# A pool that stays open into the down projection, two activation tiles loaded as a weight unit, and stores moved later

## The chip, the core and the metric

The kernel runs on one core of one Trainium2 chip. The metric is the time of one execution in device microseconds (us), and the kernel before and the changed kernel are compared by the median of several runs.

## What is computed

One layer of a diffusion backbone over 1024 tokens of width 1024, all in 32-bit floats. Three token mixers run side by side, are merged and projected, and a gated MLP with a depthwise convolution follows. The change concerns the second half only:

```python
x_mix = x + m_lat[:, :, 2] * merge_branches(ya, yb, yc, gates, w_branch[l], w_out[l])
h = rms_norm(x_mix, norm_ffn[l]) * (1.0 + m_lat[:, :, 4]) + m_lat[:, :, 3]
x = x_mix + m_lat[:, :, 5] * conv_ffn(h, w_up[l], w_dw[l], b_dw[l], w_down[l])
# conv_ffn: a, g = split(dwconv(h @ w_up)); return (a * silu(g)) @ w_down
return rms_norm(x, norm_final)
```

The MLP is 2816 wide, that is 22 tiles of 128 channels. Its activation `a * silu(g)` is a 2816 x 1024 array.

## The kernel before

Every large product is made of three products: a 32-bit operand is split into a high part (a cast on ScalarE) and a low part (source minus high part, a subtraction on VectorE), and TensorE multiplies high by high, high by low and low by high. One such matmul has 512 columns.

A weight unit (`w_unit`, L166) is one 512 KB load into a raw tile `wr`, the cast to `wh` and the subtraction to `wl`. Each of the three tags has a ring of three buffers, so a unit waits for the release of the unit three places before it. All loads and stores are issued by one engine, SyncE (SP), in the order of its queue: an issue that waits holds back all issues behind it.

The code is written in program order; a scheduler of the framework puts each engine's instructions into an order at build time. It takes the ready instruction of the smallest number, numbers rise with the program order, and `tc.high_priority(offset=n)` makes an instruction count as n places earlier. An SBUF pool is a stretch of memory, opened on a stack at the left or the right side; a tile of a new pool waits for the tiles that lay on its bytes before (`reuse_waits="tile"`).

The stages that matter here, in order:

- Merge and output projection (`merge_up`, `wo_half`, L656): two halves of 512 tokens. `wo_half` loads the residual tile `xr` (ring of two), adds, stores `xm_d`, and sums squares. `h_tile` makes the normalised input `blk["11"]`, `["21"]`, `["12"]`, `["22"]` on the right side (pool `f2`).
- Up projection (L726 to L844). Tiles f = 0 and 1 are plain, tiles 2 to 21 take seven half-size products (`up_first`, `up_rest`) with sums of the input, `T1`, `T2`, `T3` (pool `tp`, left side, which also holds the convolution's weights `cw`). `act_out` (L686) applies the convolution, SiLU and the gate to one tile: ScalarE L695, VectorE L701, L704, ScalarE L708, VectorE L711. Its operands and results are tiles of tag `c`, a ring of five in the pool `pc`, four for each f. At its end L712 stores the tile to DRAM (`act_d`).
- Down projection (L896 to L957). Pool `p2` is opened where `tp` and `pc` lay, and pool `pa` where the inputs of the up projection lay. `act` (L858) loads one half tile of 512 tokens from `act_d` into `st` (ring of four) and splits it into one of 25 `ac` tiles. The loop runs over two token halves tb, two halves of output channels mh (the last part is done apart, L929 on), 11 weight units f2_ and two tiles in each. A pair f2_ takes 24 matmuls (L871 to L873). The residual `xt` is loaded at the start of each tb.

Of the kernel before, what the change touches and what calls it, by code (L numbers as in the profile page):

```python
# [9 lines left out]
F32 = mybir.dt.float32  # L10
F32R = mybir.dt.float32r
# [7 lines left out]
P = 128  # L19
D = 1024  # L20
KT = D // P
# [9 lines left out]
FT = D_FF // P  # L31
# [6 lines left out]
NC = 5  # L38
# [4 lines left out]
WPRIO = 60  # L43
CTX_POOL = (('v', 1), ('b', 2), ('v', 2), ('b', 3), ('v', 3))
WPRIO_C = 30
WM = 8
WAT = 2
MPRIO = 100
# [43 lines left out]
def build(tc, ins, out, dbg=None):  # L92
    nc = tc.nc
    V, A, G, T, SP = nc.vector, nc.scalar, nc.gpsimd, nc.tensor, nc.sync
    with ExitStack() as top:
# [68 lines left out]
        wprio = [0]  # L164

        def w_unit(src, nk, ncol, lo_eng=None):  # L166

            cnt[0] += 1
            n = nk * ncol
            with tc.high_priority(offset=wprio[0]):  # L170
                raw = wp.tile([P, 1024], F32, tag="wr", name=f"wr{cnt[0]}", bufs=WR)
                SP.dma_start(raw[:, :n], src)
                hi = wp.tile([P, 1024], F32R, tag="wh", name=f"wh{cnt[0]}", bufs=WH)
                lo = wp.tile([P, 1024], F32R, tag="wl", name=f"wl{cnt[0]}", bufs=WL)
                A.copy(hi[:, :n], raw[:, :n])  # L175
                (lo_eng or V).tensor_tensor(out=lo[:, :n], in0=raw[:, :n], in1=hi[:, :n].bitcast(F32),  # L176
                                            op=ALU.subtract)
            return (hi[:, :n].rearrange("p (k n) -> p k n", k=nk),
                    lo[:, :n].rearrange("p (k n) -> p k n", k=nk))
# [440 lines left out]
        with ExitStack() as sm:  # L620
            mp = Aligned(sm.enter_context(tc.tile_pool(name="mp", bufs=2, reuse_waits="tile")))
            merge_up(nc, mp, ins, gate_d, y_d, xm, half, w_unit, gemm_cm, mm2)
        tss = ExitStack()
        tp = Aligned(tss.enter_context(tc.tile_pool(name="tp", bufs=1, reuse_waits="tile")))
        cw = tp.tile([P, 2 * FT, 4], F32, tag="cw", name="cw")
        SP.dma_start(cw, ins["conv"])

        for nm in ("T3", "T1", "T2"):
            blk[nm] = tuple(tp.tile([P, KQ, LH], F32R, tag=f"{nm}{p}", name=f"{nm}{p}") for p in "hl")
        ffs = ExitStack()  # L630
        ff = Aligned(ffs.enter_context(tc.tile_pool(name="ff", bufs=2, reuse_waits="tile")))

# [23 lines left out]
        def wo_half(hf):  # L656

            cols = slice(hf * LH, hf * LH + LH)
            ss = []
            for i in range(KT):  # L660
                w = w_unit(ins["w_out"][i], KT, P)
                z = bank("b", f"wo{hf}{i}", (P, 512))
                for k2 in range(2):
                    gemm_cm(z, [p[:, k2 * KQ:(k2 + 1) * KQ] for p in w], blk["12"[k2] + "12"[hf]], slice(0, LH),
                            first=k2 == 0, last=k2 == 1)
                xr = ff.tile([P, 512], F32, tag="o", name=f"xr{hf}{i}", bufs=2)
                SP.dma_start(xr, ins["xT"][i * P:(i + 1) * P, cols])
                V.scalar_tensor_tensor(out=xm[i][:, cols], in0=z, scalar=mods[:, 0, i:i + 1], in1=xr,
                                       op0=ALU.mult, op1=ALU.add)
                if i > 0:  # L670
                    SP.dma_start(xm_d[hf, i - 1], xm[i - 1][:, cols])
                sumsq(ff, ss, xm[i][:, cols], i, f"m{hf}", 512, 4)
            SP.dma_start(xm_d[hf, KT - 1], xm[KT - 1][:, cols])
            return rms_row(ff, ss, 512, f"m{hf}", "a")
# [3 lines left out]
            h_tile(k, 0, rp)  # L678
        rp = wo_half(1)
        ffs.close()  # L680
        pcs = ExitStack()
        pc = Aligned(pcs.enter_context(tc.tile_pool(name="pc", bufs=1, reuse_waits="tile")))
        P1 = [None]


        def act_out(f, cc_):  # L686

            us = []
            for s in (1, 0):
                c_ = s * FT + f  # L690
                u = pc.tile([P, L], F32, tag="c", name=f"u{f}{s}", bufs=NC)
                o = 0
                for z in cc_[s]:
                    n = z.shape[-1]
                    A.activation(u[:, o:o + n], z, AF.Identity, scale=cw[:, c_, 1:2], bias=cw[:, c_, 3:4])  # L695
                    o += n
                o = 0
                for z in cc_[s]:
                    n = z.shape[-1]
                    e = min(n, L - 1 - o)  # L700
                    V.scalar_tensor_tensor(out=u[:, o + 1:o + 1 + e], in0=z[:, :e], scalar=cw[:, c_, 0:1],  # L701
                                           in1=u[:, o + 1:o + 1 + e], op0=ALU.mult, op1=ALU.add)
                    e = 0 if o else 1
                    V.scalar_tensor_tensor(out=u[:, o + e - 1:o + n - 1], in0=z[:, e:], scalar=cw[:, c_, 2:3],  # L704
                                           in1=u[:, o + e - 1:o + n - 1], op0=ALU.mult, op1=ALU.add)
                    o += n
                if s:
                    A.activation(u, u, AF.Silu)  # L708
                us.append(u)
            g_, a_ = us  # L710
            V.tensor_tensor(out=a_, in0=a_, in1=g_, op=ALU.mult)  # L711
            SP.dma_start(act_d[f], a_)  # L712

        def plain(zs, ws, hf, ks):
# [26 lines left out]
        for k in range(KQ):  # L741
            h1, h2 = xm[k], xm[k + KQ]
            b = {nm: [p[:, k] for p in blk[nm]] for nm in ("T1", "T2", "T3")}
            V.tensor_tensor(out=h1[:, t1], in0=h1[:, t2], in1=h1[:, t1], op=ALU.subtract)
            split(b["T1"], h1[:, t1])
            V.tensor_tensor(out=h1[:, t2], in0=h2[:, t2], in1=h1[:, t2], op=ALU.subtract)
            split(b["T3"], h1[:, t2])
            V.tensor_tensor(out=h2[:, t2], in0=h2[:, t2], in1=h1[:, t1], op=ALU.subtract)
            split(b["T2"], h2[:, t2])
            V.tensor_tensor(out=h2[:, t1], in0=h2[:, t1], in1=h2[:, t2], op=ALU.subtract)  # L750
        act_out(1, za)

        blk["T4"] = blk["12"]
# [54 lines left out]
            return z  # L808

        def up_rest(f, z, w):  # L810
            p1 = P1[0]
            ca, cg = (pc.tile([P, L], F32, tag="c", name=f"c{s}{f}", bufs=NC) for s in range(2))
            p5 = ca[:, t2]
            p7 = cg[:, t2]

            def keep(out, src):
                with tc.high_priority(offset=KPRIO):
                    A.copy(out, src)

            sn = p1.tile([P, LH], F32, tag="sn", name=f"p1_{f}", bufs=2)  # L820
            keep(sn, z[:, 0])
            c = bank("a", f"upc{f}", (P, LH))
            prod(c, w["S3"], blk["T3"])
            keep(p7, c)
            V.tensor_tensor(out=ca[:, t1], in0=z[:, 1], in1=sn, op=ALU.add)
            d = bank("b", f"upd{f}", (P, LH))
            prod(d, w["S1"], blk["T1"])
            keep(p5, d)
            prod(z[:, 0], w["S2"], blk["T2"], first=False)
            u2 = p1.tile([P, LH], F32, tag="sn", name=f"u2_{f}", bufs=2)  # L830
            keep(u2, z[:, 0])
            prod(c, w["22"], blk["T4"], first=False)
            prod(d, w["S4"], blk["22"], first=False)
            G.tensor_tensor(out=cg[:, t2], in0=p7, in1=p5, op=ALU.add)
            V.tensor_tensor(out=cg[:, t2], in0=cg[:, t2], in1=u2, op=ALU.add)
            V.tensor_tensor(out=cg[:, t1], in0=c, in1=u2, op=ALU.add)  # L836
            V.tensor_tensor(out=ca[:, t2], in0=d, in1=u2, op=ALU.add)
            act_out(f, [[ca], [cg]])

        for f in range(2, FT):  # L840
            w = w_pair(f)
            w_sums(f, *w)
            z = up_first(f, w)
            up_rest(f, z, w[0])  # L844
        p1s.close()
        pcs.close()
        tss.close()
        f2s.close()

# [2 lines left out]
        p2 = Aligned(top.enter_context(tc.tile_pool(name="p2", bufs=1, reuse_waits="tile")))  # L852

        NRIGHT = 16
        NRING = 25
        acts = {}

        def act(tb, f):  # L858
            if (tb, f) not in acts:
                n = tb * FT + f  # L860
                j = n % NRING
                t = (pa if j < NRIGHT else p2).tile([P, 2, LH], F32R, tag=f"ac{j}", name=f"ac{tb}_{f}")
                with tc.high_priority(offset=APRIO):
                    raw = p2.tile([P, LH], F32, tag="st", name=f"st{tb}_{f}", bufs=4)
                    SP.dma_start(raw, act_d[f][:, tb * LH:(tb + 1) * LH])
# [28 lines left out]
                             xt[:, 2 * k2:2 * k2 + 2, o % LH:o % LH + n])  # L894

        norm = None  # L896
        act(0, 0)
        for tb in range(2):
            xt = p2.tile([P, KT, LH], F32, tag="xt", name=f"xt{tb}", bufs=2)
            for i in range(KT):  # L900
                SP.dma_start(xt[:, i], xm_d[tb, i])
            ss = []
            for mh in range(2):
                if tb == 1 and mh == 1:
# [6 lines left out]
                for f2_ in range(FT // 2):  # L911
                    w = w_unit(ins["w_down"][mh * (FT // 2) + f2_], 2, 512)
                    for f1 in range(2):
                        f = f2_ * 2 + f1
                        h = act(tb, f)
                        for j in range(4):
                            dn(zs[j], [p[:, f1] for p in w], slice(j * P, (j + 1) * P), h, f == 0, f == FT - 1)
                    if norm is not None and f2_ == 2:
                        norm = [rms_r(p2, norm[1], LH, "f0", True), norm[0]]
                    if norm is not None and f2_ == 4:  # L920
# [580 lines left out]
```

## Time and profile before

| what | us |
|---|---|
| median of 3 runs | 2192.55 |
| lowest and highest of them | 2187.08 and 2196.15 |
| the profiled execution, its own time | 2193.44 |
| its span, first to last instruction | 2191.7 |
| TensorE busy in it | 2095.4 (96%) |
| VectorE busy | 1467.9 (67%) |
| ScalarE busy | 1007.5 (46%) |

The span is the stretch that the profile draws; the execution's own time is 1.74 us longer. Matmuls overlap in the pipeline, so TensorE that is "busy" says nothing on its own: the distance from one matmul's start to the next tells its pace, and the idle stretches before an instruction, with what ended them, tell who held it up. The granted clock of TensorE (PEclk) is 1.00 at 2.4 GHz and 0.50 at 1.2 GHz.

### The profile page before, as it was taken

The numbers are of one execution on the slowest core, as the hardware profiler recorded it, in microseconds if no ns is written. First come the engines' busy times: TensorE is split into PE (matmuls) and PEld (weight loads), VectorE is DVE, ScalarE is ACT, GpSimd is POOL, SyncE is SP. The second block draws the span as 40 slices with busy tenths as digits, with TensorE's granted clock in tenths as the row PEclk, the third lists the DMA queues.
The fourth block names the chain that finished last, engine by engine and source line by source line (L and its number), as shares of the span: only waits on it lengthen the run. The fifth ranks groups of instructions, "written<-read, shape, count | busy, mean of one in ns | idle before, by whom it ended". The sixth has DMA issues, their size and how long they took to land. (4 is left out here: it accounts for less than half of the span.)

```text
span 2191.7 us, 31143 instructions
## 1 busy us (share of the span) xinstructions
PE 2095.4 (96%) x11690; PEld 1737.6 (79%) x11690; DVE 1467.9 (67%) x2593; ACT 1007.5 (46%) x1811; POOL 440.4 (20%) x390
## 2 busy tenths in 40 slices
PE   7789999999999999999999999999999999989997
PEld 3778788889998888877777788877788888768887
DVE  6946566636666687689999856559777777654333
ACT  4523323321122777677777733346444444443322
POOL 1420010001022122132333200012533344100010
PEclk9999999999999999999999999999999999989999
DMA  7420110126653211211110264551322222284343
GB/s 310 129 68 30 49 39 30 54 72 200 199 162 117 90 57 41 80 56 34 30 32 25 94 201 145 176 163 50 104 79 87 82 80 80 87 281 158 108 128 91
DMA packets 94071, 224.60 MB, mean 102 GB/s; under 512 B 10592, under 2 KB 35680, under 8 KB 92896
## 3 DMA queue, kind: packets, MB, share of 16 engines
q1 hardware_dynamic: 93632, 222.55, 31.1%
q8 instruction: 92, 1.51, 0.3%
q14 instruction: 59, 0.48, 0.1%
q10 hardware_dynamic: 288, 0.07, 0.0%
HBM read 176.96 MB, written 45.61 MB: 102 GB/s over the span
## 5 line engine op out<-in xcount | busy, mean ns | idle before, releaser
L176 DVE TENSOR_TENSOR wl<-wr,wh 128x1024 fp32r<-128x1024 f32 x147 | 186.3, 1268 | 250.3 <-ACT wh L175 248.7
L175 ACT CAST wh<-wr 128x1024 fp32r<-128x1024 f32 x152 | 158.6, 1045 | 417.0 <-PE dn L872 83.2
L1244 DVE TENSOR_TENSOR pl<-pp,ph 128x512 fp32r<-128x512 f32 x236 | 158.8, 683 | 9.6 <-ACT ph L1243 8.3
L190 PE MATMUL gz<-hh,wh 128*128 128x512 f32 x384 | 156.4, 408 | 2.9 <-ACT gs L487 2.8
L1243 ACT CAST ph<-pp 128x512 fp32r<-128x512 f32 x236 | 136.2, 584 | 43.7 <-PE pp L1239 40.8
L192 PE MATMUL gz<-hh,wl 128*128 128x512 f32 x384 | 151.9, 396 | 0.0
L191 PE MATMUL gz<-hl,wh 128*128 128x512 f32 x384 | 151.8, 395 | 0.0
L871 PE MATMUL dn<-ac,wh 128*128 128x512 f32 x264 | 103.9, 393 | 11.8 <-ACT ac L646 11.8
L201 PE MATMUL tm<-wl,hh 128*128 128x256 f32 x384 | 108.9, 283 | 2.5 <-DVE wl L176 2.5
L200 PE MATMUL tm<-wh,hh 128*128 128x256 f32 x384 | 108.7, 283 | 0.0
L202 PE MATMUL tm<-wh,hl 128*128 128x256 f32 x384 | 108.6, 283 | 0.0
L1233 PE MATMUL po<-ph,VHL 128*128 128x512 f32 x236 | 104.9, 445 | 1.3 <-ACT ph L1243 1.3
L1234 PE MATMUL po<-pl,VHL 128*128 128x512 f32 x236 | 98.8, 419 | 7.5 <-DVE pl L1244 7.3
L872 PE MATMUL dn<-ac,wh 128*128 128x512 f32 x264 | 103.6, 392 | 0.0
L873 PE MATMUL dn<-ac,wl 128*128 128x512 f32 x264 | 103.4, 392 | 0.0
L1239 PEld LDWEIGHTS pp<-ident,plat 128*128 128x128 f32 x512 | 61.1, 140 | 34.5 <-DVE pl L1244 22.1
L1239 PE MATMUL pp<-ident,plat 128*128 128x128 f32 x512 | 78.2, 275 | 10.3 <-DVE pl L1244 9.3
L190 PEld LDWEIGHTS gz<-hh,wh 128*128 128x128 f32 x384 | 72.8, 190 | 17.2 <-ACT gs L487 5.0
L695 ACT ACTIVATE u<-c,cw 128x1024 f32<-128x1024 f32 x40 | 49.8, 1246 | 76.4 <-DVE c L836 45.3
L192 PEld LDWEIGHTS gz<-hh,wl 128*128 128x128 f32 x384 | 72.5, 189 | 15.4
L191 PEld LDWEIGHTS gz<-hl,wh 128*128 128x128 f32 x384 | 72.8, 190 | 11.6
L781 POOL TENSOR_TENSOR s<-wr 128x512 f32<-128x512 f32 x20 | 30.7, 1534 | 231.7 <-DVE ws2l L647 21.5
(1496 smaller groups left out, 6278.9 us busy)
## 6 DMA issues: line engine op xcount, KB each, us to landing
wr<-in_w_cm SPq DMA_DIRECT2D x56, 512.0 KB, 3.7
wr<-in_w_up SPq DMA_DIRECT2D x44, 512.0 KB, 3.5
wr<-in_w_down SPq DMA_DIRECT2D x33, 512.0 KB, 3.5
wmr<-in_w_mod SPq DMA_DIRECT2D x32, 512.0 KB, 4.6
gate_d<-gs SPq DMA_DIRECT2D x48, 256.0 KB, 2.4
sgt<-gate_d SPq DMA_DIRECT2D x24, 512.0 KB, 3.4
act_d<-u SPq DMA_DIRECT2D x22, 512.0 KB, 2.6
st<-act_d SPq DMA_DIRECT2D x44, 256.0 KB, 4.3
```

Source lines behind the costliest of these rows:

```text
L175: A.copy(hi[:, :n], raw[:, :n])
L176: (lo_eng or V).tensor_tensor(out=lo[:, :n], in0=raw[:, :n], in1=hi[:, :n].bitcast(F32), op=ALU.subtract)
L190: T.matmul(psl, wh[:, k, c], hh[:, k0 + k, cols], start=s, stop=False)
L191: T.matmul(psl, wh[:, k, c], hl[:, k0 + k, cols], start=False, stop=False)
L192: T.matmul(psl, wl[:, k, c], hh[:, k0 + k, cols], start=False, stop=e)
L200: T.matmul(psl, hh[:, k, toks], wh[:, k % 4, :], start=s, stop=False)
L201: T.matmul(psl, hh[:, k, toks], wl[:, k % 4, :], start=False, stop=False)
L202: T.matmul(psl, hl[:, k, toks], wh[:, k % 4, :], start=False, stop=e)
L1233: T.matmul(po, vv, ph, start=n == 0, stop=False)
L1239: T.transpose(pp[:, h], PT(h, n), ident)
L1243: A.copy(ph, pp)
L1244: V.tensor_tensor(out=pl, in0=pp, in1=ph.bitcast(F32), op=ALU.subtract)
```

## The change

- `pc` is opened at the start of the output projection, ahead of `ff`, and closed at the end of the kernel only. It now holds `cw`, the ring `c` and the tiles `sn`, which lay in `tp` and `p1`. `tp` is opened after `ff` is closed and holds `T1`, `T2` and `T3` alone. So `p2` lies over `tp` and no longer over `cw` and the tiles of the last `act_out`.
- Five of the 25 `ac` tiles are taken from the ring `c`.
- The ring of `xr` grows from two to six.
- The store of an activation tile is split off (`act_store`): it stands in the next tile's turn, after `up_first`, and that of the last tile in the down projection after its second pair.
- The first two half tiles are one `w_unit` of 512 KB in the ring of the weights, ahead of the first down unit. They serve the first pass (tb 0, mh 0); for mh 1 they are loaded by `act` again.
- The weight units count as 30 places earlier, not 60, until the third pair is done.
- The loads of `xt` stand after the pairs 4 to 7 of mh 0, two at each.

```diff
@@ w_unit
-                SP.dma_start(raw[:, :n], src)
+                SP.dma_start(raw[:, :n] if len(src.shape) == 2 else raw[:, :n].rearrange("p (k n) -> p k n", k=nk), src)
@@ build
-        tss = ExitStack()
-        tp = Aligned(tss.enter_context(tc.tile_pool(name="tp", bufs=1, reuse_waits="tile")))
-        cw = tp.tile([P, 2 * FT, 4], F32, tag="cw", name="cw")
+        pcs = top.enter_context(ExitStack())
+        pc = Aligned(pcs.enter_context(tc.tile_pool(name="pc", bufs=1, reuse_waits="tile")))
+        cw = pc.tile([P, 2 * FT, 4], F32, tag="cw", name="cw")
         SP.dma_start(cw, ins["conv"])
-
-        for nm in ("T3", "T1", "T2"):
-            blk[nm] = tuple(tp.tile([P, KQ, LH], F32R, tag=f"{nm}{p}", name=f"{nm}{p}") for p in "hl")
@@ wo_half
-                xr = ff.tile([P, 512], F32, tag="o", name=f"xr{hf}{i}", bufs=2)
+                xr = ff.tile([P, 512], F32, tag="o", name=f"xr{hf}{i}", bufs=6)
@@ after wo_half(1)
         ffs.close()
-        pcs = ExitStack()
-        pc = Aligned(pcs.enter_context(tc.tile_pool(name="pc", bufs=1, reuse_waits="tile")))
+        tss = ExitStack()
+        tp = Aligned(tss.enter_context(tc.tile_pool(name="tp", bufs=1, reuse_waits="tile")))
+
+        for nm in ("T3", "T1", "T2"):
+            blk[nm] = tuple(tp.tile([P, KQ, LH], F32R, tag=f"{nm}{p}", name=f"{nm}{p}") for p in "hl")
         P1 = [None]
+        pend = []
@@ act_out
             V.tensor_tensor(out=a_, in0=a_, in1=g_, op=ALU.mult)
+            pend.append((f, a_))
+
+        def act_store():
+
+            f, a_ = pend.pop(0)
             SP.dma_start(act_d[f], a_)
@@ before act_out(1, za)
+        act_store()
         act_out(1, za)
@@ up_rest
-            sn = p1.tile([P, LH], F32, tag="sn", name=f"p1_{f}", bufs=2)
+            sn = pc.tile([P, LH], F32, tag="sn", name=f"p1_{f}", bufs=2)
...
-            u2 = p1.tile([P, LH], F32, tag="sn", name=f"u2_{f}", bufs=2)
+            u2 = pc.tile([P, LH], F32, tag="sn", name=f"u2_{f}", bufs=2)
@@ loop over f
             z = up_first(f, w)
+            act_store()
             up_rest(f, z, w[0])
         p1s.close()
-        pcs.close()
         tss.close()
@@ act
+        NLEFT = 4
...
-                t = (pa if j < NRIGHT else p2).tile([P, 2, LH], F32R, tag=f"ac{j}", name=f"ac{tb}_{f}")
+                if j < NRIGHT + NLEFT:
+                    t = (pa if j < NRIGHT else p2).tile([P, 2, LH], F32R, tag=f"ac{j}", name=f"ac{tb}_{f}")
+                else:
+                    t = pc.tile([P, 2, LH], F32R, tag="c", name=f"ac{tb}_{f}", bufs=NC)
@@ down projection
-        act(0, 0)
+
+        a0 = w_unit(act_d[0:2, :, :LH].rearrange("f p t -> p f t"), 2, LH)
+        first = [(a0[0][:, f], a0[1][:, f]) for f in range(2)]
+        wprio[0] = WPRIO_D
         for tb in range(2):
             xt = p2.tile([P, KT, LH], F32, tag="xt", name=f"xt{tb}", bufs=2)
-            for i in range(KT):
-                SP.dma_start(xt[:, i], xm_d[tb, i])
...
-                        h = act(tb, f)
+                        h = first.pop(0) if first else act(tb, f)
                         for j in range(4):
                             dn(zs[j], [p[:, f1] for p in w], slice(j * P, (j + 1) * P), h, f == 0, f == FT - 1)
+                    if pend and f2_ == 1:
+                        act_store()
+                    if mh == 0 and f2_ in (4, 5, 6, 7):
+                        for i in range(2 * f2_ - 8, 2 * f2_ - 6):
+                            SP.dma_start(xt[:, i], xm_d[tb, i])
+                    if tb == mh == 0 and f2_ == 2:
+                        wprio[0] = WPRIO
```

## Rows read from the trace of the kernel before

**Rows 1.** Windows of core 0: busy time per engine, PEclk, DMA share, GB/s.
```profile
1915.60:1927.56 11.96, 0.14 (x2) 0.00 (x1) 6.41 (x7) 2.89 (x4) 0.00 (x0) 0.62 0.36 109
1927.56:2112.90 185.34, 185.25 (x820) 153.04 (x820) 81.24 (x95) 65.86 (x88) 11.70 (x8) 0.99 0.56 182
...
1925.00:1930.00 5.00, 2.44 (x5) 1.71 (x6) 1.85 (x3) 2.40 (x4) 0.00 (x0) 0.50 0.87 277
1930.00:1935.00 5.00, 5.00 (x19) 3.98 (x19) 1.49 (x3) 0.69 (x2) 0.00 (x0) 0.79 0.97 338
```

**Rows 2.** TensorE's waits, whole span: total us, times, longest.
```profile
PE dn L871 <- ACT ac L646: 11.8, 1, 11.8
...
PE up L799 <- DVE c L825: 3.3, 3, 1.6
...
PE wo L190 <- DVE xm L668: 2.3, 1, 2.3
```

**Rows 3.** Chain that ended last, around 1920 us: start, us, what.
```profile
1915.12 1.28 DVE u L701
...
1921.08 1.24 DVE u L711
1922.33 0.33 SPq L712
1922.75 4.12 DMA st<-act_d
1926.89 0.63 ACT ac L646
```

**Rows 4.** Timeline of TensorE: start, us, instruction, tiles, [idle before and its end].
```profile
1904.47 0.39 PE L801 MATMUL upc<-T3h,vlS 128*128 128x512 f32 x1
...
1909.91 0.39 PE L801 MATMUL up<-T2h,ws21l 128*128 128x512 f32 x1
...
1915.35 0.39 PE L801 MATMUL upd<-B22h,vlS 128*128 128x512 f32 x1
1927.56 0.80 PE L871 MATMUL dn<-ac,wh 128*128 128x512 f32 x1 [11.82 <-ACT ac L646]
...
1932.20 0.39 PE L872 MATMUL dn<-ac,wh 128*128 128x512 f32 x1
```

**Rows 5.** Timeline of SP's queue: start, us, line, transfer, count.
```profile
1863.40 0.33 SPq L172 DMA_DIRECT2D wr<-in_w_down  x1
...
1904.43 8.35 SPq L172 DMA_DIRECT2D wr<-in_w_down  x2
...
1946.61 0.42 SPq L901 DMA_DIRECT2D xt<-xm_d  x1
```

**Rows 6.** Timeline of ScalarE: the first and third down unit's cast.
```profile
1891.07 1.05 ACT L175 CAST wh<-wr 128x1024 fp32r<-128x1024 f32 x1 [2.10 <-PE up L800]
...
1910.11 1.05 ACT L175 CAST wh<-wr 128x1024 fp32r<-128x1024 f32 x1 [1.91 <-PE up L800]
```

**Rows 7.** Tile st: its subtractions, ns shortest/median/longest, first to last start.
```profile
L647 DVE TENSOR_TENSOR ac<-st,ac x44: 678/692/715, 1927.5 to 2042.3; 128x512 fp32r<-128x512 f32 x44
```

**Rows 8.** TensorE in the output projection, around its wait of 2.35 us.
```profile
1446.24 0.50 PE L190 MATMUL wo<-B12h,wh 128*128 128x512 f32 x1 [2.35 <-DVE xm L668]
...
1448.00 0.63 PE L190 MATMUL wo<-B12h,wh 128*128 128x512 f32 x1
1448.42 0.63 PE L191 MATMUL wo<-B12l,wh 128*128 128x512 f32 x1
```

**Rows 9.** Up projection: SP's stores and loads, and VectorE's write into ring c.
```profile
1559.41 0.33 SPq L712 DMA_DIRECT2D act_d<-u  x1
...
1586.51 0.33 SPq L768 DMA_DIRECT2D wr<-in_w_up  x1
...
1579.64 0.69 DVE L825 TENSOR_TENSOR c<-up,p 128x512 f32<-128x512 f32 x1
```

**Rows 10.** Page, DMA issues: KB each, median us to landing.
```profile
act_d<-u SPq DMA_DIRECT2D x22, 512.0 KB, 2.6
```

More of the change, by code (lines that the diff above doesn't have):

```diff
@@ L45 @@
 WPRIO_C = 30
+WPRIO_D = 30
 WM = 8
@@ L810, in up_rest @@
         def up_rest(f, z, w):
-            p1 = P1[0]
             ca, cg = (pc.tile([P, L], F32, tag="c", name=f"c{s}{f}", bufs=NC) for s in range(2))
```

## The prediction

> **What bounds the kernel now.** I read the stages first, then who waited, then the chain of work that ended last, and only then single engines. In the down projection TensorE is busy for 185.25 of 185.34 us, and just ahead of it stands a hole: from 1915.60 to 1927.56 it does 0.14 us of work in 11.96 [rows 1]. The list of TensorE's waits gives the same hole as one wait of 11.8 us for the split of an activation tile (`ac`), its largest single wait; in the up projection it waits only 3.3 us, in three pieces, and in the output projection once, 2.3 us [rows 2]. So this place is bound by a latency and everything around it by TensorE's own matmuls.
>
> The chain tells what the hole is made of [rows 3]. The last tile's `act_out` runs on VectorE from 1915.12 to 1922.32, its store is issued at 1922.33, the loads of `st` follow it on SP's queue at 1922.75 and land 4.12 us later, ScalarE casts in 0.63, and TensorE starts. The first tile that is loaded is f = 0, which was stored some 400 us earlier: nothing in its data needs this chain. Two things hold it: the order on SP, where the store stands ahead, and the memory, since `p2` lies over `cw`, which the last L704 reads.
>
> **What the hole costs.** Matmuls in the up projection start every (1909.91 - 1904.47) / 24 = 0.227 us [rows 4]. The last one starts at 1915.35, so the next could start at 1915.58; it starts at 1927.56: 11.98 us. Then the clock: over the hole the granted clock is 0.62 on average, from 1925 to 1930 it is 0.50, the lower level of 1.2 GHz, and from 1930 to 1935 0.79 [rows 1]. The eleventh down matmul starts at 1932.20, 4.64 us after the first, where ten steps at full pace are 2.27: 2.37 us lost [rows 4]. Together 14.35 us.
>
> Here the Trainium skill ("TensorE: Matmul & The Clock Gate", the section on the HAM clock gate) says that the reduced clock is the resting state and that sustained work lifts it; by that rule the 2.37 us go with the hole, and the trace agrees, as the clock is 0.99 over the whole down projection, the slow start included [rows 1].
>
> **Part by part.** *The first pair as a weight unit.* It takes the place in the weight rings that the first down unit has today, and that unit was loaded at 1863.40 and cast at 1891.07; the third was cast at 1910.11 in 1.05 us [rows 5, 6]. So the tile pair is split by about 1894, the first and second down units by about 1904 and 1913 (the places of today's second and third), all ahead of 1915.58. That its load reads DRAM which SP wrote is no wait: tiles 0 and 1 were stored hundreds of us earlier, and today the load of tile 0 is issued 0.4 us after the store of tile 21 without waiting for it to land [rows 3]. TensorE can go on at 1915.58.
>
> *What is late next.* A pair is 24 matmuls, 24 x 0.227 = 5.45 us. So tiles 2 and 3 are due at 1921.0, tile 4 and the third down unit at 1926.5. Tiles 2 to 5 go through `st`, which now lies over the `T` tiles, whose last reads are at 1904.47 (`T3`), 1909.91 (`T2`) and, for `T1`, between the two [rows 4]. So their loads can be issued from about 1910.4, land by 1914.5 at today's 4.12, and be split by ScalarE at 0.63 and VectorE at 0.69 each [rows 3, 7], 1917 to 1918. The third down unit now needs the ring place of the pair that is in use until 1921.0: cast 1.05, subtraction about as long as L711's 1.24 (the same 1024 columns), so 1923.4 at best. VectorE is the tight one: `act_out` fills it from 1915.12 to 1922.32; four subtractions of tiles (2.8) and two of weights (2.5) come on top, so the work needed by 1926.5 (2.1 for three tiles, 1.24 for one unit) ends near 1925.7 if it all stands behind `act_out`. Cover 0.8 us for that unit, and none for tile 2 if its subtraction is behind L711. I take no stall, since tile 2 counts 60 places earlier than it stands and its data can be there by 1914.5.
>
> *Stores later, `xt` later.* A store leaves SP's queue 0.4 us shorter ahead of the loads; nothing in the up projection waits for SP today, so I count nothing. The `xt` loads (16 x 256 KB) are moved back in program order, but the order on SP is the scheduler's: today a second-half `xt` is loaded at 1946.61, over 100 us ahead of its turn [rows 5]. Their place over `T3` and `T1` is free earlier than that of `st`. If eight of them and the weights issued at 1904.43 go first, that is 2.6 MB, at the 338 GB/s of the fullest window [rows 1] 7.7 us, until 1912.2; four `st` tiles (1 MB, 3.1 us) then land by 1915.3. With all sixteen first it is 1921.5: a stall of 1 to 2 us. So between nothing and 2; I take nothing.
>
> *The rest.* Tiles 0 and 1 are loaded and split once more for mh 1: 2 x (0.63 + 0.69) on ScalarE and VectorE, which are busy 65.86 and 81.24 us of 185.34 there [rows 1]; hidden. Six `xr` places: the adds that read them wait for TensorE and VectorE, so nothing. `sn` and `c` at other addresses: nothing, as long as VectorE's order stays. The reordering can move the waits of 2.3 and 3.3 us [rows 2] either way, with the clock's share 4 us at most.
>
> **Sum.** 2193.44 - 14.35 = 2179.1 on the profiled execution's own time. It stands 0.9 above the median of 2192.55, which would give 2178.2; with some tenths for the thin cover on VectorE I say 2179.0.
>
> **Rivals.**
>
> *B: the hole moves one pair on and is small.* Tile 2 is subtracted behind L711: ready at 1922.32 + 0.69 = 1923.0, due 1921.2 with its second matmul, stall 1.8. The clock may fall for it: in the output projection a wait of 2.35 us was followed by matmuls 0.42 apart, eight of them, so 8 x 0.2 = 1.6 us more [rows 8]. 2180.8 to 2182.5. The same Trainium skill page has it as practical advice that only longer idle stretches matter; here the trace differs, with those 2.35 us. For it: VectorE's fill. Against it: the priority. 0.16.
>
> *C: the last store still stands ahead of the loads of `st` on SP.* Then tile 2 comes as tile 0 does today, TensorE waits from 1921.0 to 1927.56, 6.5 us, and up to 2.37 for the clock: saved 5.5 to 7.8, so 2185.6 to 2188. The Trainium skill ("DMA: Bandwidth & Descriptors", on the anatomy of one DMA) says that a wait happens on the issuing sequencer, not in the DMA engine; the trace agrees, with loads issued 0.4 us after the store that waited. Against it: in program order and priority the store is now behind the first two `act` pairs. 0.08.
>
> *D: it does not do what it says*, as the pair's load is held until the last store: 2192.5. Against it the rings above. 0.04.
>
> *E: the order ahead of the up projection shifts*, by its 4 us either way: 2175 to 2183. 0.07.
>
> *F, slower: a store that comes too late holds the ring `c`.* The tile `ca` of f + 2 takes the place of the result of f. Today a store is issued at 1559.41, lands 2.6 us later, and VectorE writes into the place at 1579.64 [rows 9, 10]: some 17 us of cover. It decides once the store is issued over 17 us later than now, as behind a weight load like that of 1586.51, which waits for a ring place: then 1586.8 + 2.6 - 1579.6 = 10 us per tile, and for 18 tiles 180 us, 2359; two such tiles are enough to end at 2199. Against it: the next tile's turn starts soon after the result is there. 0.05.
>
> **How the numbers follow.** The forecast has 0.60. A change of 0.5% is 11.0 us, about what a measurement of this kernel can tell, so faster means under 2181.6. Faster: the forecast, half of B, most of E: 0.60 + 0.08 + 0.05 = 0.73. Slower: F, 0.05. The rest, 0.22, is no change. The range runs from 2174, E's better end, to 2187, most of C; it leaves out D, F and part of C, 0.13.
>
> **What would show it.** Right: the first down matmul 0.23 us after the last up matmul, the granted clock 1.00 through the seam, the pair's cast near 1891, the `st` loads ahead of the last store on SP, and TensorE's largest remaining wait elsewhere. B: a wait of `dn` for a subtraction behind L711. C: the store first on SP. E: other waits of `wo` and `up`. F: waits of `up` for the ring `c`, and an up projection longer than 388 us. I would be wrong if `xt` loads crowd in ahead of `st`, or if VectorE's queue puts the weights ahead of tile 2.

## The result, and the profile after

The changed kernel takes 2179.95 us (median of 5 runs, 2175.43 to 2181.9) against 2192.55 (5 runs, 2187.08 to 2196.15; the three of the table ahead are among them): a ratio of 0.9942, 95% interval 0.9923 to 0.9962, so 12.6 us or 0.58% less. The forecast was 2179.0. The profiled execution of the changed kernel has an own time of 2175.43, the fastest of the five, with a span of 2173.6.

The two profiled spans differ by 18.1 us, more than the change can claim: the first matmul of the output projection starts at 1386.5 before and at 1380.3 after, and ahead of it nothing is changed. Other executions of the changed kernel and its variants start it between 1380 and 1388. So the traces are compared from that matmul on, by the starts of TensorE's matmuls (us; "seam" is from the last up matmul to the first down matmul; dl is the last part of the down projection; the two short steps into the up projection and into dl, 1.02 and 0.62 us in both kernels, have no row and are in the sum):

| stage | before | after | difference |
|---|---|---|---|
| output projection | 93.93 | 93.93 | 0 |
| up projection | 433.93 | 436.22 | +2.29 |
| seam | 12.21 | 0.23 | -11.98 |
| down projection | 184.86 | 182.75 | -2.11 |
| dl | 65.65 | 65.65 | 0 |
| first to last | 792.23 | 780.43 | -11.80 |

The seam is where the forecast put it. TensorE's timeline in the changed kernel, from the last up matmuls to the second pair (start, us, line, matmul, tiles, shape):

```profile
1911.47 0.39 PE L810 MATMUL upd<-B22h,vlS 128*128 128x512 f32 x1
1911.70 0.39 PE L883 MATMUL dn<-wh,wh 128*128 128x512 f32 x1
...
1917.14 0.61 PE L883 MATMUL dn<-ac,wh 128*128 128x512 f32 x2
1917.77 0.50 PE L884 MATMUL dn<-ac,wh 128*128 128x512 f32 x1
...
1918.34 0.39 PE L883 MATMUL dn<-ac,wh 128*128 128x512 f32 x1
```

The first down matmul follows the last up matmul by one ordinary step of 0.23 us, where [rows 4] had 12.21. Its operands are both weight tiles (`wh`), the pair that was loaded as a unit. The second pair reads `ac`, and there four steps of TensorE take 1.20 us (1917.14 to 1918.34) where four ordinary ones take 0.91: a stall of 0.29 us is left. The windows of the changed kernel (columns as in [rows 1]) show no dip of the clock:

```profile
1911.70:2095.00 183.30, 183.13 (x821) 151.50 (x819) 88.03 (x102) 68.94 (x92) 11.64 (x8) 1.00 0.58 194
...
1910.00:1915.00 5.00, 5.00 (x24) 4.14 (x23) 3.57 (x4) 2.99 (x3) 0.00 (x0) 1.00 0.89 297
```

TensorE is busy throughout at a granted clock of 1.00, where [rows 1] had 0.62 over the hole and 0.50 behind it. SP's queue of the changed kernel shows what moved:

```profile
1859.55 0.38 SPq L173 DMA_DIRECT2D wr<-act_d  x1
...
1900.57 8.34 SPq L173 DMA_DIRECT2D wr<-in_w_down  x2
1909.00 1.81 SPq L877 DMA_DIRECT2D st<-act_d  x4
1910.85 2.29 SPq L935 DMA_DIRECT2D xt<-xm_d  x4
...
1920.08 0.32 SPq L720 DMA_DIRECT2D act_d<-u  x1
```

The pair is loaded at 1859.55, 52 us ahead of its use; four `st` loads are issued at 1909.00, 11 us ahead of the last store (1920.08), which in [rows 3] stood ahead of them.

What got worse is in the up projection. TensorE's waits of the changed kernel (total us, times, longest) have no row for `dn` any more, and this one for `up`, beside 3.3, 3 and 1.6 in [rows 2]:

```profile
PE up L808 <- DVE c L833: 3.4, 2, 2.1
```

That row hardly grew, though the stage grew by 2.29 us. The experiments ask first where that difference comes from, and then what each part of the change is worth.

### The profile page after: what moved, and what is told of

Its sections match the earlier page's. It is cut to its first block, busy times and chain, and to the rows that moved or that the text cites. A ratio compares the mean times of both kernels' runs of the same rounds, so it can differ in the third digit from the quotient of the medians.

```text
span 2173.6 us, 31141 instructions
## 1 busy us (share of the span) xinstructions
PE 2088.8 (96%) x11690; PEld 1734.6 (80%) x11690; DVE 1469.9 (68%) x2594; ACT 1007.3 (46%) x1812; POOL 438.9 (20%) x390
## 5 line engine op out<-in xcount | busy, mean ns | idle before, releaser
L177 DVE TENSOR_TENSOR wl<-wr,wh 128x1024 fp32r<-128x1024 f32 (+1 forms) x148 | 187.7, 1269 | 237.3 <-ACT wh L176 233.4
L884 PE MATMUL dn<-ac,wh 128*128 128x512 f32 x256 | 99.7, 390 | 0.0
L883 PE MATMUL dn<-ac,wh 128*128 128x512 f32 x256 | 99.6, 390 | 0.0
L202 PEld LDWEIGHTS tm<-wl,hh 128*128 128x128 f32 x384 | 73.7, 192 | 3.4 <-DVE wl L177 3.0
```

The costliest lines, as they stand in the source:

```text
L202: T.matmul(psl, hh[:, k, toks], wl[:, k % 4, :], start=False, stop=False)
L883: T.matmul(z, w[0][:, c], h[0], start=s, stop=False)
L884: T.matmul(z, w[0][:, c], h[1], start=False, stop=False)
```

## The experiments

Each is the changed kernel with one edit, except the weight unit alone, which is the kernel before with one part of the change. The stages are those of the table above.

**The changed kernel again**, beside the others on one chip.

> The changed kernel once more, beside the next two. I compare stages by their matmuls: output projection to last matmul of the down projection took 792.2 us before and 780.4 in the changed kernel, of which the up projection 433.9 and 436.2. If the 2.3 us that the up projection grew by come from the code, they stand again here: up 436.2, sum 780.4. If they were chance, up is 434 here.

Measured: 2181.72 (ratio 0.995, 0.9937 to 0.9962), 10.1 us under the 2191.85 of the kernel before in this comparison. Stages: up projection 436.25, seam 0.23, down 182.76. So the 2.3 us in the up projection belong to this program and are no accident of one execution. The sum is 778.89 and not 780.4, since the output projection took 92.36 here: TensorE's wait of 2.37 us there was not followed by a fall of the granted clock (the last section).

**The `sn` tiles back in the pool `p1`.** In the change they moved to `pc`, so `p1` shrank by two tiles of 2 KB for each partition.

```diff
-            sn = pc.tile([P, LH], F32, tag="sn", name=f"p1_{f}", bufs=2)
+            sn = P1[0].tile([P, LH], F32, tag="sn", name=f"p1_{f}", bufs=2)
...
-            u2 = pc.tile([P, LH], F32, tag="sn", name=f"u2_{f}", bufs=2)
+            u2 = P1[0].tile([P, LH], F32, tag="sn", name=f"u2_{f}", bufs=2)
```

> The tiles sn go back into p1; the rest of the change stays. Theory: without sn, p1 is 4 KB smaller and begins 4 KB higher, so that s34 lies over xm2 and no longer over xm1; GpSimd's sums of f = 2 wait for it and then run beside VectorE's busiest stretch and slow it. With sn back, the sums run as before: up projection 433.9 (2.3 us less than in the changed kernel), sum 778.1, median about 2177.6. Rival: the growth comes from the later stores or from the new place of tp and pc: up 436.2, sum 780.4, as in the changed kernel.

Measured: 2177.22 (0.9925, 0.9911 to 0.9938), 14.6 us under the 2191.85 of the kernel before in the same comparison. Up projection 433.56, seam 0.23, down 182.75, sum 777.79. The stage is 2.66 us shorter than in the changed kernel, 0.37 shorter than in the kernel before, and this version is faster than both.

**4 KB of unused memory at the end of `p1`**, so that its tiles stand where they stood, while `sn` stays in `pc`.

```diff
+            if f == 2:
+                P1[0].tile([P, L], F32, tag="pad", name="pad")
             sn = pc.tile([P, LH], F32, tag="sn", name=f"p1_{f}", bufs=2)
```

> sn stays in pc as in the changed kernel, but p1 gets an unused tile of 4 KB where sn stood. Theory (addresses of s12 and s34 over xm): as with sn back, up projection 433.9, sum 778.1. Rival (it is sn's own place in pc that matters): up 436.2, sum 780.4.

Measured: 2177.45 (0.9928, 0.9916 to 0.9941); up projection 433.56, sum 777.81. A tile that nothing reads or writes gives the same as `sn_back`: it isn't where `sn` lies, but where the others come to lie.

**The same 4 KB at the start of `p1`**: the pool has its old size, but its first working tiles stand 4 KB higher.

```diff
             with tc.high_priority(offset=wprio[0]):
+                if f == 2:
+                    p1.tile([P, L], F32, tag="pad", name="pad")
                 s12 = p1.tile([P, 2, KQ * P], F32, tag="s12", name=f"s12_{f}")
```

> As the run pad, but the unused 4 KB are the first tile of p1 and not the last, so p1 has its old size and s12 and s34 lie over xm1 and xm2 as in the changed kernel. Theory (the addresses decide): GpSimd's second sum of f = 2 waits some 12 us again, the up projection takes 436.2 to 437.4, the sum of the stages is 780.4 to 781.8. Rival (p1's size or start decides): up 433.6, sum 777.8.

Measured, in one execution: 2179.51, up projection 436.27, sum 780.57. With the size restored and the addresses shifted, the lost time is there again.

The chain is to be seen in GpSimd's timeline. `w_sums` of f = 2 computes four sums into `s12` and `s34`, the first tiles of `p1`. With `sn` gone from it, `p1` starts 4 KB higher; the addresses are worked out from the sizes of the tiles, and the waits below fit them. So `s12` lies on the place of `xm[0]` before and on that of `xm[1]` after, and `s34` on `xm[1]` before and on `xm[2]` after. `xm` is what VectorE's split of the input (L741 on) reads for k = 0, 1, 2 in turn. First the variant with `sn` back (as in the kernel before, the first sum waits 15.10 us):

```profile
1502.10 5.29 POOL L790 TENSOR_TENSOR s<-wr 128x512 f32<-128x512 f32 x1 [15.10 <-DVE T3l L646]
1507.33 2.29 POOL L796 TENSOR_TENSOR s<-wr,wr 128x512 f32<-128x512 f32 x1
```

Then the changed kernel:

```profile
1499.22 1.29 POOL L790 TENSOR_TENSOR s<-wr 128x512 f32<-128x512 f32 x1 [19.31 <-DVE T3l L646]
1512.92 3.48 POOL L796 TENSOR_TENSOR s<-wr,wr 128x512 f32<-128x512 f32 x1 [12.41 <-DVE T3l L646]
```

The first sum waits for the `T3l` of k = 1 in place of k = 0, and the second waits another 12.41 us for that of k = 2. (With the 4 KB first, the same two rows read 19.31 and 12.41.) So this sum and the two behind it now run beside the last part of VectorE's split. VectorE of the changed kernel there:

```profile
1515.83 1.12 DVE L756 TENSOR_TENSOR xm<-xm,xm 128x512 f32<-128x512 f32 x1
1516.88 1.78 DVE L646 TENSOR_TENSOR T3l<-xm,T3h 128x512 fp32r<-128x512 f32 x1
1518.59 1.78 DVE L758 TENSOR_TENSOR xm<-xm 128x512 f32<-128x512 f32 x1
...
1534.78 0.68 DVE L833 TENSOR_TENSOR c<-up,p 128x512 f32<-128x512 f32 x1
```

and with `sn` back:

```profile
1522.70 0.68 DVE L756 TENSOR_TENSOR xm<-xm,xm 128x512 f32<-128x512 f32 x1
1523.30 0.68 DVE L646 TENSOR_TENSOR T3l<-xm,T3h 128x512 fp32r<-128x512 f32 x1
1523.90 0.68 DVE L758 TENSOR_TENSOR xm<-xm 128x512 f32<-128x512 f32 x1
```

Three operations take 4.68 us in place of 2.04, so 2.64 us are lost. The delay runs on through both engines. Counted from the first up matmul (1475.25, and 1482.34 with `sn` back), VectorE's subtraction of `ws2` ends at 53.95 in place of 51.27; GpSimd's sums of f = 3 wait for it and start at 54.08 in place of 51.40. At L833 of f = 2 part of the delay has gone (from L756 to L833 it is 18.95 us in place of 17.82, see the last section), but at L833 of f = 3 it is whole again: 82.41 in place of 79.70. TensorE waits for both, f = 2 and f = 3. Changed kernel:

```profile
1535.51 0.62 PE L808 MATMUL up<-T2h,ws2h 128*128 128x512 f32 x1 [2.12 <-DVE c L833]
...
1538.92 0.51 PE L810 MATMUL up<-T2h,ws2l 128*128 128x512 f32 x1
...
1557.71 0.50 PE L808 MATMUL up<-T2h,ws3h 128*128 128x512 f32 x1 [1.25 <-DVE c L833]
```

and with `sn` back:

```profile
1541.25 0.50 PE L808 MATMUL up<-T2h,ws2h 128*128 128x512 f32 x1 [1.61 <-DVE c L833]
...
1562.09 0.50 PE L808 MATMUL up<-T2h,ws3h 128*128 128x512 f32 x1 [1.50 <-DVE c L833]
```

So TensorE starts L808 of f = 3 at 82.46 in place of 79.75, 2.71 us late, and the stage is 2.66 us longer: VectorE's delay sets it. The list of waits hardly shows this, since the wait of f = 2 grew by 0.5 us and that of f = 3 shrank by 0.25. In between, the eight steps behind the wait of 2.12 us take 3.41 us (1535.51 to 1538.92), 0.43 each, where eight ordinary ones are 1.82: 1.6 us more, at a reduced clock. The windows behind the wait of f = 2 (columns as in [rows 1]), changed kernel first, then with `sn` back:

```profile
1535.51:1538.92 3.41, 3.41 (x9) 2.62 (x9) 1.83 (x2) 2.91 (x5) 1.75 (x2) 0.53 0.21 31
...
1541.25:1544.60 3.35, 3.35 (x15) 2.77 (x16) 3.35 (x3) 1.98 (x4) 2.10 (x2) 1.00 0.58 99
```

These 1.6 us are no cost of their own: TensorE would otherwise have waited longer at f = 3. The variant with the weight units 60 places ahead (below) shows it. It has the same wait at f = 2, a granted clock of 1.00 behind it, and a longer wait at f = 3:

```profile
1540.64 0.50 PE L808 MATMUL up<-T2h,ws2h 128*128 128x512 f32 x1 [2.12 <-DVE c L833]
...
1562.86 0.50 PE L808 MATMUL up<-T2h,ws3h 128*128 128x512 f32 x1 [2.86 <-DVE c L833]
```

From one L833 to the next VectorE takes 22.22 us there and 22.21 in the changed kernel, with the clock's fall and without.

**The ring of `xr` back to two.**

```diff
-                xr = ff.tile([P, 512], F32, tag="o", name=f"xr{hf}{i}", bufs=6)
+                xr = ff.tile([P, 512], F32, tag="o", name=f"xr{hf}{i}", bufs=2)
```

> The ring of xr is two again. The prediction gave this part nothing: output projection 93.9 us as in both kernels, sum 780.4. Rival: the larger ring hides a wait that the new places would bring; then the output projection grows.

Measured, in one execution: 2183.47; output projection 93.92, seam 0.23, down 182.75, up projection 437.31, sum 781.53. Six places are worth nothing in the stage that uses them. (For the 1.1 us in the up projection see the last section.)

**Without the weight unit**: tiles 0 and 1 come through `act` as before.

```diff
-        a0 = w_unit(act_d[0:2, :, :LH].rearrange("f p t -> p f t"), 2, LH)
-        first = [(a0[0][:, f], a0[1][:, f]) for f in range(2)]
+        first = []
+        act(0, 0)
```

> The changed kernel, but tiles 0 and 1 go through st as before. Theory: the loads of st are issued some 2.5 us before the last up matmul, land 4.1 later and are cast in 0.6, so the hole is about 2.5 us, with the clock's fall 1.6 more at most: sum of the stages 782.5 to 785. Rival: the open pool alone does it all, 780.4; or tile 0 still waits for act_out's end, 792.

Measured: 2187.41 (0.9983, 0.9973 to 0.9992 against 2191.77), 4.4 us faster than before; seam 4.56, down 185.49, up 436.22. SP, ScalarE, VectorE and TensorE of this variant:

```profile
1912.77 1.81 SPq L877 DMA_DIRECT2D st<-act_d  x4
...
1918.20 1.06 ACT L711 ACTIVATE u<-u 128x1024 f32<-128x1024 f32 x1
1919.16 2.16 ACT L645 CAST ac<-st 128x512 fp32r<-128x512 f32 x4
...
1919.60 1.28 DVE L707 SCALAR_TENSOR_TENSOR u<-c,cw,u 128x1023 f32<-128x1023 f32 x1
1920.80 2.49 DVE L646 TENSOR_TENSOR ac<-st,ac 128x512 fp32r<-128x512 f32 x4
...
1919.81 1.22 PE L883 MATMUL dn<-ac,wh 128*128 128x512 f32 x2 [4.17 <-ACT ac L645]
```

The loads are issued 2.5 us ahead of the last up matmul (1915.25). Then the cast stands behind the SiLU of the last `act_out` on ScalarE and the subtraction behind its L707 on VectorE. So the open pool takes the store and the memory out of the way, but the split still queues with `act_out`: a hole of 4.6 us, and behind it a granted clock of 0.50 until 1925. That is more than was expected, a hole of about 2.5 us and a sum of 782.5 to 785: the sum is 787.34, and the queues of ScalarE and VectorE were the part left out.

**The weight unit alone**, in the kernel before, with its pools, its store and its `xt` loads.

```diff
...
-        act(0, 0)
+        a0 = w_unit(act_d[0:2, :, :LH].rearrange("f p t -> p f t"), 2, LH)
+        first = [(a0[0][:, f], a0[1][:, f]) for f in range(2)]
...
-                        h = act(tb, f)
+                        h = first.pop(0) if first else act(tb, f)
```

> The kernel before with the first pair as a weight unit and nothing else. Theory (two halves: the unit removes the first wait, the open pool keeps the next one away): TensorE goes on at once into the first pair, then waits for tile 2, whose load on SP stands behind the last store and two weight loads: a wait of 6.5 to 9 us after 24 matmuls and a clock spell, so 10 to 11 us of the 14.35 stay; sum of the stages 788 to 790. Rival: the unit alone does it all, 780 to 778.

Measured: 2190.14 (0.9992, 0.9983 to 1.0002): not told from no change. SP and TensorE:

```profile
1920.48 0.33 SPq L712 DMA_DIRECT2D act_d<-u  x1
1921.62 1.46 SPq L172 DMA_DIRECT2D wr<-in_w_down  x2
1923.18 1.33 SPq L865 DMA_DIRECT2D st<-act_d  x3
...
1918.93 0.39 PE L873 MATMUL dn<-wh,wl 128*128 128x512 f32 x1
1929.61 0.80 PE L871 MATMUL dn<-ac,wh 128*128 128x512 f32 x1 [10.29 <-ACT ac L646]
```

The hole moves behind the pair: 24 matmuls, then 10.68 us. The pair covers 5.45 us, but the chain grew. Two weight loads now stand between the last store and the `st` loads, so these are issued 9.69 us after the last up matmul (1913.49) in place of 7.40 [rows 3, 4], and the first matmul that needs them starts 16.12 us after it in place of 12.21. 5.45 less 3.91 is 1.54 us, all that was gained of a hole of 11.98. The sum is 790.48, slightly over the 788 to 790 expected.

**The stores back at the end of `act_out`**, at once.

```diff
-            pend.append((f, a_))
-
-        def act_store():
-
-            f, a_ = pend.pop(0)
             SP.dma_start(act_d[f], a_)
...
-            act_store()
...
```

> The changed kernel with each store at the end of its act_out, as before. The prediction gave later stores nothing. Theory: on SP the loads of st still stand ahead of the last store, since their place is free earlier: sum 780.4. Rival C of the prediction: the last store stands ahead of them, a hole of 6.5 us and the clock one pair later: 787 to 789.

Measured: 2180.29 (0.9944, 0.993 to 0.9959). On SP the last store still stands behind the `st` loads:

```profile
1916.05 1.81 SPq L870 DMA_DIRECT2D st<-act_d  x4
...
1927.13 0.32 SPq L715 DMA_DIRECT2D act_d<-u  x1
```

Seam 0.23, down 182.75, as in the change; up projection 436.74, sum 780.89. So the store's place in the program did not decide the order on SP. With the old pools (the weight unit alone) the last store stood ahead of the `st` loads, with the open pool it stands behind them.

**The `xt` loads back at the start of each tb.**

```diff
             xt = p2.tile([P, KT, LH], F32, tag="xt", name=f"xt{tb}", bufs=2)
+            for i in range(KT):
+                SP.dma_start(xt[:, i], xm_d[tb, i])
...
-                    if mh == 0 and f2_ in (4, 5, 6, 7):
-                        for i in range(2 * f2_ - 8, 2 * f2_ - 6):
-                            SP.dma_start(xt[:, i], xm_d[tb, i])
```

> The changed kernel with the xt loads at the start of each token half, as before. In the order built, three st loads stand ahead of eight xt loads and the load of tile 5 behind them. Theory: tiles 2 and 3 come as in the changed kernel; eight loads of 256 KB take about 6.2 us at 338 GB/s, so tile 5 lands about 1921 on the changed kernel's clock, due 1925: no stall, sum 780.4. Rival: 1 to 2 us lost behind the xt loads, 782.

Measured: 2181.24 (0.9948, 0.9934 to 0.9963); seam 0.23, down 182.90. Here eight `xt` loads (2 MB) do go between the `st` loads:

```profile
1916.95 1.34 SPq L877 DMA_DIRECT2D st<-act_d  x3
1918.33 5.55 SPq L916 DMA_DIRECT2D xt<-xm_d  x8
1924.26 4.09 SPq L877 DMA_DIRECT2D st<-act_d  x4
```

and cost 0.15 us. The up projection is 437.37 (see the last section) and the sum 781.75. That this is near the rival's 782 does not support the rival, since only 0.15 us is lost behind the `xt` loads.

**The weight units 60 places ahead all along.**

```diff
-WPRIO_D = 30
+WPRIO_D = 60
```

> The changed kernel with the first down units at 60 places as the others. In the order built TensorE, ScalarE and GpSimd are the same; on VectorE the third down unit's subtraction stands ahead of the last gate product L714 and of tile 5, on SP one weight load ahead of the last store. Theory: the unit is due 10.9 us after the last up matmul and its cast is done about 7.0 us after it, so nothing is lost: seam 0.23 us, down projection 182.75, sum 780.4 to 781.8. Rival: tile 5 or the store come late and TensorE waits 1 us or more in the first four pairs.

Measured, in one execution: 2180.48; seam 0.23, down 182.75, up projection 436.80, sum 780.86. The smaller lead of the weights is worth nothing in the down projection.

## Why the prediction was right, step by step

**The hole, 11.98 us: as predicted, to the hundredth.** The seam went from 12.21 to 0.23. The pair's cast stands at 1887.20, 24 us ahead of its use (forecast: split by about 1894, some 22 us ahead of 1915.58).

**The clock, 2.37 us: right.** The down projection is 2.11 us shorter, which is 2.37 less the stall at tile 2 (0.29) within 0.03. The clock is 1.00 through the seam, so the rule of the Trainium skill that the prediction cites ("TensorE: Matmul & The Clock Gate", on the HAM clock gate) agrees with the trace: work without a hole kept the clock up.

**Tile 2, "no stall": wrong by 0.29 us, with two of its numbers off.** I had the `st` loads issued at 1910.4 on my time axis, 4.95 us ahead of the last up matmul at 1915.35, and landed by 1914.5. They were issued 2.47 us ahead of it (1909.00 to 1911.47), since on SP's queue they stand behind two weight loads at 1900.57, of which the second waits for a ring place; I had priced the memory under `st`, not that queue. Then ScalarE's casts stand behind L711 and VectorE's subtractions between L707 and L714. Those two engines in the changed kernel:

```profile
1914.42 1.06 ACT L711 ACTIVATE u<-u 128x1024 f32<-128x1024 f32 x1
1915.38 2.17 ACT L645 CAST ac<-st 128x512 fp32r<-128x512 f32 x4
...
1915.83 1.28 DVE L707 SCALAR_TENSOR_TENSOR u<-c,cw,u 128x1023 f32<-128x1023 f32 x1
1917.03 1.89 DVE L646 TENSOR_TENSOR ac<-st,ac 128x512 fp32r<-128x512 f32 x3
1918.83 1.22 DVE L714 TENSOR_TENSOR u<-u,u 128x1024 f32<-128x1024 f32 x1
1920.57 2.35 DVE L177 TENSOR_TENSOR wl<-wr,wh 128x1024 fp32r<-128x1024 f32 x2
```

This is rival B in a milder form: the place (VectorE, tile 2's subtraction) is right, but the subtractions went ahead of the last operation of `act_out` and not behind it, and 0.29 us took the place of 1.8 and 1.6. The third unit came off as forecast: subtracted by about 1921.8 and due at 1911.70 + 10.90 + 0.29 = 1922.9, a cover of 1.1 where I had 0.8.

**`sn` and `c` at other addresses, "nothing, as long as VectorE's order stays": the step that failed.** The order stayed: between the changed kernel and the variant with `sn` back, GpSimd and VectorE of this stretch run the same sequence. What changed is which old tile two sums must wait for, and with it what runs beside what: 2.29 us. Rival E had a loss of this size near this place, but through a reordering; the runs with 4 KB at the end and at the start of the pool show that addresses alone do it. The prediction worked out what comes to lie over the `T` tiles on the left, and not what the other tiles of `p1`, the pool on the right that `sn` leaves, come to lie on.

**The rest at nothing: right.** Stores, `xt`, ring of `xr` and the weights' lead are each worth nothing in their stages (0.15 us for `xt`). The up projection is 0.5 to 1.2 us longer in each of these four variants than in the change; each has one trace, so whether the edit or the execution does that is not shown.

**The sum.** From the first matmul of the output projection on: -11.98, -2.37, +0.29 and +2.29 make -11.8, against the -14.35 of the forecast. The measured -12.6 holds that within its interval (8.3 to 16.9 us). The variant with `sn` back has all of the forecast's mechanism and not the unforeseen 2.3: 14.6 us under the kernel before in its own comparison, and -14.4 by stages (792.23 to 777.79). So that the median of 2179.95 came within 1 us of the forecast is partly luck, from the spread of the runs; the mechanism was right, and 2.6 us of losses were missed.

**The rivals.** C is out: the last store stands 11 us behind the first `st` loads. D and F are out: the seam closed, and the up projection grew by 2.3 us, not by 10 for each tile. The two halves of the change need each other: the unit alone gives 1.6 us (not told from nothing), all but the unit 4.4, both together 10 to 12.6. No run tries the five `ac` tiles in the ring `c` apart from the rest.

## What to carry to other kernels

A wait at a change of stage often has several holders in a row (a queue's order, the memory below, the engines that split the data); list them all, since taking one away brings up the next, as the weight unit alone showed. When a tile moves to another pool, write down which old tiles every other tile of both pools now lies on, above all in pools that are opened while the work on the old tiles still runs: here 4 KB of unused memory were worth 2.7 us. Follow a delay to the last wait that it reaches before adding up what it costs: the wait that grew and the reduced clock behind it were not the bill here, the next wait was. Compare stages from a point ahead of all changed code, as 6 us of the difference of two spans here lay ahead of it.

## What the runs showed of the hardware

GpSimd's sums and VectorE's operations slow each other down, and either can be the one that yields. Where the sums of f = 3 begin beside VectorE's subtraction `vlS`, the changed kernel shows (start, us, engine)

```profile
1529.33 2.21 POOL L790 TENSOR_TENSOR s<-wr 128x512 f32<-128x512 f32 x1 [9.52 <-DVE ws2l L646]
...
1529.72 0.68 DVE L646 TENSOR_TENSOR vlS<-s,vhS 128x512 fp32r<-128x512 f32 x1
```

and the variant with early `xt` loads

```profile
1536.77 1.62 POOL L790 TENSOR_TENSOR s<-wr 128x512 f32<-128x512 f32 x1 [11.98 <-DVE ws2l L646]
...
1537.16 1.78 DVE L646 TENSOR_TENSOR vlS<-s,vhS 128x512 fp32r<-128x512 f32 x1
...
1544.25 0.80 PE L808 MATMUL up<-T2h,ws2h 128*128 128x512 f32 x1 [3.41 <-DVE c L833]
```

The same two operations meet 0.39 us apart in both; in one the sum yields, in the other the subtraction, which then takes 1.10 us longer. The kernel before and the variants with `sn` back, the 4 KB at the end or the weight unit alone are of the second kind; the change itself in both traces, the 4 KB at the start, the variant without the unit and the one with 60 places are of the first. That is why part of the 2.64 us had gone at L833 of f = 2. It came back by f = 3: the sums of f = 3 had started 2.68 us late and yielded on top of that, so VectorE waits 1.63 us for the cast of their result (`ws3`), where with `sn` back it does not wait. The ring of two, the stores at once and the early `xt` have both losses: TensorE's wait is 3.4 us there in place of 2.1, the reduced clock lasts longer behind it, and the up projection is 436.7 to 437.4 in place of 436.2. With 60 places it is 436.80 for another reason: at the earlier meeting three of VectorE's operations take 1.78 us each, 3.3 lost in place of 2.64. Elsewhere a sum took 5.29 us beside six VectorE operations that kept their 0.68.

The Trainium skill ("SBUF — State Buffer", section "Who interferes with whom") says that a VectorE instruction with two SBUF inputs contends with a GpSimd instruction that reads SBUF, and that the order of issue decides who is held up. The trace agrees on the first. On the second it does not decide: both outcomes occur with the same pair, and the starts that it shows are the same in both, GpSimd 0.39 us ahead. What decided stays open, and with it why edits that don't touch this stretch fall on one side or the other.

A wait of TensorE of the same length is followed by a fall of the granted clock in one execution and not in another. In the output projection the waits are 2.33 to 2.37 us in all twelve traces. In eleven of them the mean granted clock of the 5 us behind the wait is 0.66 to 0.69, with matmuls 0.43 us apart; in the second trace of the changed kernel it is 1.00, and the stage takes 92.36 us in place of 93.8 to 94.0. In the up projection the waits of 2.08 to 2.12 us were followed by a fall in four traces and not in the one with 60 places, and those of 1.60 and 1.61 us in none of four.
